# Token norms of the input from a second load of x with tokens on the partitions, and their factors in two multiplications

## The chip, the cores and the metric

The kernel runs on one core of a Trainium2 chip. The core has TensorE (matrix products, written PE in the profile, its weight loads PEld), VectorE (DVE), ScalarE (ACT), GpSimd (POOL) and SyncE (SP), which here only issues transfers; 16 DMA engines move data between the chip's memory and the on-chip memory of 128 partitions. Each engine works through its own queue in order and waits on semaphores. The metric is the device time of one execution in microseconds (us); the median of three runs before the change is 2240.29 us (2239.57 to 2240.89).

## The reference

One inference step of a one-layer encoder on 1024 prompt tokens and 64 sample tokens of width 1024. What matters here is its head:

```
def rms_norm(x, g=None):
    y = xf * lax.rsqrt(jnp.mean(xf * xf, axis=-1, keepdims=True) + EPS)
    ...
rq, rk, rv, rg, sq, sk, sv, ga, gb = jnp.split(rms_norm(x, g_attn) @ w_in, ...)
q, k, v = retention_qkv(rq, rk, rv, pos)          # rotary on q and k
s = einsum('bihd,bjhd->bhij', q, k) * intra       # decay inside a chunk
o = s @ v + (q @ state) * q_dec
new_state = state * exp(log_gamma * C) + (k * k_dec)^T @ v
```

Each token's row of x is divided by the root of its mean square. A projection is linear, so the kernel multiplies by the gain g_attn before the projections and applies the token's factor 1/root afterwards, where it needs it: to v and the scores of retention by token, and to the other projections as a row over all partitions. Behind the head follow the four-head retention, a sliding-window attention, two gated branches, cross attention, a SwiGLU block and a last norm.

## The kernel before

All 1088 tokens are held as columns, the 1024 features as 8 tiles of 128 partitions (KT = 8), in two halves of HALF = 544 tokens. Products are in fp32 as three passes of a high and a low part (`split`, lines 122 to 124: a cast on ScalarE, a difference on VectorE). The big projections go through one step of Strassen's scheme (`strassen`, line 247): seven products, each of four weight tiles and both quarters of a half, into pairs of PSUM banks `pq`; VectorE adds them up into `u` (line 252) and `stage` (line 571), and by that frees the banks for later products.

The order of instructions on each engine is not written out: the tile framework plans it with a timeline simulated at build time (line 94), from program order, dependencies and planned durations, with a few hints (`high_priority`, `issue_after`). SyncE's queue takes nearly all loads and stores, each with its wait for the buffer or the data in front, so a load that waits holds up those behind it.

`project_phase` (line 546) is the stage around the change. After the first product of values it opens a pool `ra`, loads the rotary table `rope`, and for the first head projects and rotates k (`rotated`, line 590: VectorE's adds at line 571, its four multiplications at lines 602 to 605, GpSimd's sum and difference at 606 and 607, stores to `d_qkv` in memory), calls `token_squares`, projects and rotates q, calls `token_roots` and `retention_setup`, and then `retention(0)` (line 702), which loads k, v and q from `d_qkv` in blocks of 256 tokens. The planner runs the projections of the next head among the retention's blocks.

- `token_squares` (line 448): for each half and each of the 8 feature tiles a load of 128 x 544 from `xT` into a tile `xsq`, whose buffers are those of four retention tiles not yet in use (tags kt, vb, ss, st); ScalarE squares it in place (line 457; the first of a half straight into `rstd`), VectorE adds it to `rstd` (line 459). After that `rstd` holds, for each token's column, 128 partial sums.
- `token_roots` (line 461): nine small products of `rstd` with ones on TensorE (line 468; the profile counts two instructions for each) turn them into a sum per token with tokens on the partitions, in `pt`; the steps of `rsqrt` (lines 289 to 294, on VectorE but for a root on ScalarE) make `rtok`, 128 x 9, in two sets, for eight columns of 128 tokens and one of 64.
- `retention_setup` (line 676): the factors of tokens for 4 heads and 2 kinds (decay of k, decay of the output), `tok`, from `rtok` and the tables `tab`: for each head and kind one multiplication for eight columns (line 684) and one for the last (line 686); one more instruction forms a square (line 688).
- `spread_roots` (line 472) later writes `rtok` as a row over all partitions into `rstd`.

In retention, `kt` (lines 730, 731) takes `tok`, `vb` (739, 740) and the scores' scaling (751) take `rtok`; the scores `pss` (line 746, three passes at lines 149 to 151) need q's load `qs`, its cast on ScalarE and its difference on VectorE.

Of the kernel before, what the change touches and what calls it, by code (L numbers as in the profile page):

```python
# [11 lines left out]
F32 = mybir.dt.float32  # L12
F32R = mybir.dt.float32r
AF = mybir.ActivationFunctionType
ALU = mybir.AluOpType
# [4 lines left out]
P = 128  # L20
D = 1024
KT = D // P
SEQ = 1024
SMP = 64
T = SEQ + SMP
# [4 lines left out]
H = 4  # L30
# [10 lines left out]
HALF = T // 2  # L41
# [68 lines left out]
class Kernel:  # L110
# [336 lines left out]

    def token_squares(self):

        nc, tags = self.nc, ("kt", "vb", "ss", "st")  # L450
        for t in range(2):
            hs = slice(t * HALF, (t + 1) * HALF)
            for k in range(KT):
                x = self.ra.tile([P, HALF], F32, tag=tags[k % 4], bufs=1, name="xsq")
                self.load(x, self.io["xT"][k, :, hs])
                acc = self.rstd[:, hs]
                nc.scalar.activation(x if k else acc, x, AF.Square)
                if k:
                    nc.vector.tensor_tensor(out=acc, in0=acc, in1=x, op=ALU.add)

    def token_roots(self):

        nc = self.nc
        ps = self.norm_psum("pt")
        pv = ps[:, :18].rearrange("p (t two) -> p t two", two=2)
        for i in range(9):
            w = P if i < 8 else SMP
            nc.tensor.matmul(pv[:w, i, :], self.rstd[:, i * P:i * P + w], self.ones[:, :2], start=True, stop=True)
        self.rsqrt(self.rtok[:, :8], pv[:, :8, 0], D)
        self.rsqrt(self.rtok[:SMP, 8:], pv[:SMP, 8:, 0], D)  # L470

    def spread_roots(self):

# [202 lines left out]
    def retention_setup(self):  # L676

        nc, tab = self.nc, self.tab
        self.load(tab[:, 0], self.io["c_kdec"])
        self.load(tab[:, 1], self.io["c_gdec"])  # L680
        for h in range(H):
            for i in range(2):
                v = lambda x: x.rearrange("p (b two) -> p b two", two=2)
                nc.vector.tensor_tensor(out=v(self.tok[:, i, h, :8]), in0=v(self.rtok[:, :8]),
                                        in1=tab[:, i, h, :2].unsqueeze(1).broadcast_to([P, 4, 2]), op=ALU.mult)
                nc.vector.tensor_tensor(out=self.tok[:, i, h, 8:], in0=self.rtok[:, 8:], in1=tab[:, i, h, 2:], op=ALU.mult)
        f = self.tok[:, 1].rearrange("p h t -> p (h t)")
        nc.vector.scalar_tensor_tensor(self.tok[:, 2].rearrange("p h t -> p (h t)"), f, 1.0 / 256, f, ALU.mult, ALU.mult)

# [1013 lines left out]
```

## Time and profile before

| | |
|---|---|
| median of the runs | 2240.29 us |
| the profiled execution | 2244.47 us, its span 2242.7 us |
| granted TensorE clock, mean | 0.988 |
| TensorE busy | 2168.9 us |
| VectorE busy | 1596.0 us |
| ScalarE busy | 885.4 us |
| GpSimd busy | 692.1 us |
| moved by DMA | 290.86 MB |

The profile follows one execution. Its page gives the busy time of each engine with the share of the span, the chain of work that ended last, and the costliest groups of instructions with the mean duration of one and the engine's idle time in front of them. Views of the trace cut it to a stretch: waits (who waited for whom: total, times, longest), instructions in order of time (start, duration, engine, line, output<-inputs), groups by line or by tile (count, shortest/median/longest in ns), and busy time by windows, whose rows give the window, its length, busy time and count of each engine, the granted clock, the DMA engines' busy share and GB/s. A name such as `xsq` is a tile of the program, L459 a line of it, SPq the sequencer that issues transfers. Consecutive instructions of one engine overlap a little, so that the step from one start to the next is shorter than the duration.

### The profile page before, as it was taken

How to read it: one execution, taken by the hardware profiler on the slowest of the kernel's cores; microseconds unless marked ns; L12 is line 12 of the kernel's file. 1: busy time of each engine (PE TensorE's matmuls, PEld its weight loads, DVE VectorE, ACT ScalarE, POOL GpSimd, SP SyncE). 2: the span in 40 equal slices, each digit the busy share in tenths (PEclk: the TensorE clock that was granted, in tenths of full speed). 3: DMA queues.
4: the chain of work that ended last, by engine and by line, in shares of the span. 5: the costliest groups of instructions: out<-in, count | busy, mean ns of one | idle time of the engine just before them, and what ended most of it. 6: DMA issues, size and time to landing. Idle time of an engine off the chain costs nothing.

```text
span 2242.7 us, 41756 instructions
## 1 busy us (share of the span) xinstructions
PE 2168.9 (97%) x16434; PEld 2105.3 (94%) x16434; DVE 1596.0 (71%) x2655; ACT 885.4 (39%) x1897; POOL 692.1 (31%) x466
## 2 busy tenths in 40 slices
PE   8899999999999989999999999999999999999986
PEld 8899999999999977779999998999999999999986
DVE  7986878666687667776455556668777677778587
ACT  7333333435444355554133333333323222344243
POOL 1441533342253112220000000014556555434462
PEclk9999999999999999999999999999999999999998
DMA  5533445443445475326443111422333332475233
GB/s 193 163 108 114 118 124 136 133 126 114 167 151 181 150 229 163 114 69 211 132 152 101 64 46 59 138 89 88 121 129 102 102 120 90 147 267 184 85 98 108
DMA packets 182599, 290.86 MB, mean 130 GB/s; under 512 B 40290, under 2 KB 110850, under 8 KB 182402
## 3 DMA queue, kind: packets, MB, share of 16 engines
q1 hardware_dynamic: 177794, 279.26, 39.3%
q10 hardware_dynamic: 4608, 8.91, 1.1%
q8 instruction: 130, 2.13, 0.4%
q14 instruction: 67, 0.55, 0.1%
HBM read 196.95 MB, written 91.16 MB: 128 GB/s over the span
## 4 chain that ended last, share of the span: by engine, by line
PE 79%; DVE 11%; DMA 5%; issue 2%; ACT 2%; POOL 1%; SPq 0%; DVEq 0%; ACTq 0%; POOLq 0%
PE pq L208 15%; PE pq L206 15%; PE pq L205 15%; PE pd L149 8%; PE pd L151 8%; PE pd L150 8%; DVE wq L124 2%; PE pout L1006 1%; DMA hl<-d_op 1%; PE pp L990 1%; PE pss L948 1%; DVE T L124 1%; DVE B L124 1%; DVE xg L1294 1%; DMA qs<-d_qkv 1%
## 5 line engine op out<-in xcount | busy, mean ns | idle before, releaser
L124 DVE TENSOR_TENSOR wq<-raw,wq 128x512 fp32r<-128x512 f32 (+1 forms) x505 | 448.8, 893 | 125.2 <-ACT wq L123 122.0
L123 ACT CAST wq<-raw 128x512 fp32r<-128x512 f32 (+1 forms) x505 | 307.5, 614 | 568.0 <-PE pq L208 259.1
L205 PE MATMUL pq<-T,wq 128*128 128x272 f32 x1832 | 492.9, 289 | 6.8 <-DVE u L252 3.6
L206 PE MATMUL pq<-T,wq 128*128 128x272 f32 x1832 | 493.0, 289 | 0.0
L206 PE MATMUL pq<-B,wq 128*128 128x272 f32 x1592 | 428.9, 289 | 9.1 <-DVE B L124 9.1
L205 PE MATMUL pq<-B,wq 128*128 128x272 f32 x1592 | 427.1, 289 | 0.2 <-ACT B L123 0.2
L208 PE MATMUL pq<-T,wq 128*128 128x272 f32 x1832 | 384.5, 290 | 3.4 <-DVE wq L124 3.4
L183 POOL TENSOR_TENSOR raw<-raw 128x512 f32<-128x512 f32 (+1 forms) x59 | 80.1, 1357 | 897.2 <-DVE rs_r L291 485.7
L205 PEld LDWEIGHTS pq<-T,wq 128*128 128x128 f32 x1832 | 346.1, 189 | 7.9 <-DVE u L252 3.7
L206 PEld LDWEIGHTS pq<-T,wq 128*128 128x128 f32 x1832 | 345.9, 189 | 0.3 <-issue 0.3
L208 PE MATMUL pq<-B,wq 128*128 128x272 f32 x1592 | 333.9, 290 | 0.0
L206 PEld LDWEIGHTS pq<-B,wq 128*128 128x128 f32 x1592 | 300.4, 189 | 11.0 <-DVE B L124 10.7
L205 PEld LDWEIGHTS pq<-B,wq 128*128 128x128 f32 x1592 | 300.2, 189 | 0.9 <-issue 0.4
L208 PEld LDWEIGHTS pq<-T,wq 128*128 128x128 f32 x1832 | 291.2, 190 | 4.6 <-DVE wq L124 3.8
L208 PEld LDWEIGHTS pq<-B,wq 128*128 128x128 f32 x1592 | 252.9, 190 | 0.5 <-issue 0.3
L252 DVE TENSOR_TENSOR u<-pq,u 128x544 f32<-128x544 f32 x177 | 127.6, 721 | 109.7 <-PE pq L208 109.2
L186 POOL TENSOR_TENSOR raw<-raw 128x512 f32<-128x512 f32 (+1 forms) x59 | 85.5, 1449 | 127.3 <-DVE wq L124 124.7
L976 POOL TENSOR_TENSOR t<-t,den 128x768 f32<-128x768 f32 (+2 forms) x34 | 47.9, 1408 | 170.7 <-DVE den L974 44.4
L571 DVE TENSOR_TENSOR stage<-pq,u 128x544 f32<-128x544 f32 x112 | 80.4, 718 | 26.4 <-PE pq L208 25.4
L184 POOL TENSOR_TENSOR raw<-raw 128x512 f32<-128x512 f32 (+1 forms) x59 | 87.3, 1480 | 3.7
L1461 POOL TENSOR_TENSOR y<-u,y 128x544 f32<-128x544 f32 x38 | 62.6, 1656 | 72.6 <-DVE y L1459 50.5
L189 POOL TENSOR_TENSOR raw<-raw 128x512 f32<-128x512 f32 (+1 forms) x59 | 83.3, 1412 | 4.4
(373 smaller groups left out, 4677.0 us busy)
## 6 DMA issues: line engine op xcount, KB each, us to landing
hl<-d_op SPq DMA_DIRECT2D x85, 272.0 KB, 4.6
d_qkv<-stage SPq DMA_DIRECT2D x44, 272.0 KB, 2.3
d_op<-stage SPq DMA_DIRECT2D x44, 272.0 KB, 2.4
d_op<-ht SPq DMA_DIRECT2D x44, 272.0 KB, 3.3
raw<-w_gate SPq DMA_DIRECT2D x22, 512.0 KB, 3.5
raw<-w_up SPq DMA_DIRECT2D x22, 512.0 KB, 3.6
d_gate<-stage ACTq DMA_DIRECT2D x32, 272.0 KB, 2.7
raw<-w_down SPq DMA_DIRECT2D x16, 512.0 KB, 4.2
```

Source lines behind the costliest of these rows:

```text
L123: self.last_cast = self.nc.scalar.copy(hi, src).ins
L124: return self.nc.vector.tensor_tensor(out=lo, in0=src, in1=hi.bitcast(F32), op=ALU.subtract).ins
L149: mm(ps, wh, xh, start=start, stop=False)
L150: mm(ps, wh, xl, start=False, stop=False)
L151: self.last_mm = mm(ps, wl, xh, start=False, stop=stop).ins
L184: tt(out=a21, in0=a21, in1=a22, op=add)
L186: tt(out=a11, in0=a22, in1=a11, op=sub)
L189: tt(out=a12, in0=a12, in1=a11, op=sub)
L205: mm(ps[:, c, :HC], w[:, 0, ks], x[:, 0, cs], start=start, stop=False)
L206: mm(ps[:, c, :HC], w[:, 0, ks], x[:, 1, cs], start=False, stop=False)
L208: self.last_mm = mm(ps[:, c, :HC], w[:, 1, ks], x[:, 0, c * HC:(c + 1) * HC], start=False, stop=stop).ins
L252: add = lambda out, a, b: nc.vector.tensor_tensor(out=out, in0=a, in1=b, op=ALU.add)
```

## The change

The host hands x over a second time, untransposed (`x_tok`, 1088 x 1024). `token_squares` loads it in nine tiles with tokens on the partitions, 128 x 1024 (the last has 64 tokens), in three buffers (tags kt, vb, st; the one of ss is too small for 1024 columns). ScalarE squares each in place and writes the sum over its columns into a column of `rtok`. The adds on VectorE and the products with ones are gone, and `rstd` is first written by `spread_roots`. `token_roots` is one set of root steps over the nine columns, in place (in the last column the 64 lanes without a token hold 1.0 from line 350 and are not used). `retention_setup` forms the factors of both kinds and all heads in one multiplication for eight columns and one for the last.

```diff
     def token_squares(self):
 
-        nc, tags = self.nc, ("kt", "vb", "ss", "st")
-        for t in range(2):
-            hs = slice(t * HALF, (t + 1) * HALF)
-            for k in range(KT):
-                x = self.ra.tile([P, HALF], F32, tag=tags[k % 4], bufs=1, name="xsq")
-                self.load(x, self.io["xT"][k, :, hs])
-                acc = self.rstd[:, hs]
-                nc.scalar.activation(x if k else acc, x, AF.Square)
-                if k:
-                    nc.vector.tensor_tensor(out=acc, in0=acc, in1=x, op=ALU.add)
+        tags = ("kt", "vb", "st")
+        for i in range(9):
+            w = min(P, T - i * P)
+            x = self.ra.tile([P, D], F32, tag=tags[i % 3], bufs=1, name="xsq")[:w]
+            self.load(x, self.io["x_tok"][i * P:i * P + w])
+            self.nc.scalar.activation(x, x, AF.Square, accum_out=self.rtok[:w, i:i + 1])
 
     def token_roots(self):
 
-        nc = self.nc
-        ps = self.norm_psum("pt")
-        pv = ps[:, :18].rearrange("p (t two) -> p t two", two=2)
-        for i in range(9):
-            w = P if i < 8 else SMP
-            nc.tensor.matmul(pv[:w, i, :], self.rstd[:, i * P:i * P + w], self.ones[:, :2], start=True, stop=True)
-        self.rsqrt(self.rtok[:, :8], pv[:, :8, 0], D)
-        self.rsqrt(self.rtok[:SMP, 8:], pv[:SMP, 8:, 0], D)
+        self.rsqrt(self.rtok, self.rtok, D)
...
         self.load(tab[:, 0], self.io["c_kdec"])
         self.load(tab[:, 1], self.io["c_gdec"])
-        for h in range(H):
-            for i in range(2):
-                v = lambda x: x.rearrange("p (b two) -> p b two", two=2)
-                nc.vector.tensor_tensor(out=v(self.tok[:, i, h, :8]), in0=v(self.rtok[:, :8]),
-                                        in1=tab[:, i, h, :2].unsqueeze(1).broadcast_to([P, 4, 2]), op=ALU.mult)
-                nc.vector.tensor_tensor(out=self.tok[:, i, h, 8:], in0=self.rtok[:, 8:], in1=tab[:, i, h, 2:], op=ALU.mult)
+        n = 2 * H
+        tok, tab = (x.rearrange("p i h t -> p (i h) t") for x in (self.tok[:, :2], tab))
+        nc.vector.tensor_tensor(out=tok[:, :, :8].rearrange("p n (b two) -> p n b two", two=2),
+                                in0=self.rtok[:, :8].rearrange("p (b two) -> p b two", two=2).unsqueeze(1).broadcast_to([P, n, 4, 2]),
+                                in1=tab[:, :, :2].unsqueeze(2).broadcast_to([P, n, 4, 2]), op=ALU.mult)
+        nc.vector.tensor_tensor(out=tok[:, :, 8], in0=tab[:, :, 2], in1=self.rtok[:, 8:].broadcast_to([P, n]), op=ALU.mult)
...
     arr["xT"] = np.ascontiguousarray(x.T).reshape(KT, P, T)
+    arr["x_tok"] = x
```

## The prediction, made before the changed kernel was run

> **What bounds the kernel now.** I read the page first: the shares of the engines, then the chain that ended last.
>
> ```profile
> PE 2168.9 (97%) x16434; PEld 2105.3 (94%) x16434; DVE 1596.0 (71%) x2655; ACT 885.4 (39%) x1897; POOL 692.1 (31%) x466
> ...
> PE 79%; DVE 11%; DMA 5%; issue 2%; ACT 2%; POOL 1%; SPq 0%; DVEq 0%; ACTq 0%; POOLq 0%
> ```
>
> TensorE works 2168.9 of 2242.7 us, so only 74 us of it stand still, and an edit on another engine is worth at most the TensorE waits that it removes. Which waits lie where the change works shows in the busy time by windows: the stretch from the first loads of xsq to the first retention block, the two long holes in it with the time right behind each, and the rest of the retention stage.
>
> ```profile
> 55.00:125.00 70.00, 61.58 (x468) 60.84 (x468) 66.74 (x108) 26.43 (x47) 33.32 (x20) 0.95 0.45 144
> 77.60:81.20 3.60, 0.00 (x0) 0.00 (x0) 3.60 (x5) 1.14 (x2) 1.71 (x1) 1.00 1.00 338
> 82.00:85.30 3.30, 3.30 (x17) 3.30 (x16) 3.30 (x6) 1.82 (x3) 1.42 (x1) 0.51 0.92 322
> 111.25:114.70 3.45, 0.00 (x0) 0.00 (x0) 1.18 (x2) 0.61 (x2) 2.28 (x2) 1.00 0.34 99
> 116.20:119.60 3.40, 3.40 (x19) 3.40 (x18) 3.40 (x7) 0.45 (x1) 1.56 (x1) 0.50 0.11 15
> 115.00:575.00 460.00, 453.56 (x3598) 443.07 (x3598) 343.66 (x618) 193.05 (x416) 158.47 (x106) 1.00 0.42 123
> ```
>
> The columns are the window, its length, the busy time of PE, PEld, DVE, ACT and POOL, the granted clock, the DMA share and GB/s. Between 55 and 125 us VectorE is busy 66.74 of 70 us and TensorE misses 8.42. Behind each hole of some 3.5 us the granted clock is 0.51 and 0.50 for 3.3 and 3.4 us, so a hole costs another 3.3 x 0.49 = 1.6 and 3.4 x 0.50 = 1.7 us. In the 460 us after that TensorE misses only 6.4. The waits of TensorE in this stretch, from the view of waits:
>
> ```profile
> PE pq L205 <- DVE u L252: 3.6, 1, 3.6
> PE pss L149 <- ACT qs L123: 3.5, 1, 3.5
> PE pq L205 <- DVE stage L571: 0.6, 1, 0.6
> PE pk L699 <- issue: 0.6, 1, 0.6
> ```
>
> These four are the whole 8.42 us (3.6 + 3.5 + 0.6 + 0.6). The first is VectorE being late; in the chain of waits cut to the first 240 us the adds that the change removes are a line of their own, and in VectorE's order of time the late instruction stands right behind them:
>
> ```profile
> by line: PE pq L208 9.4%; PE pq L205 9.3%; PE pq L206 9.1%; issue 6.9%; DVE wq L124 4.9%; DMA xr<-xT 4.2%; DVE rstd L459 4.1%; DVE xg L1294 3.5%; DVE T L124 3.4%; DMA qs<-d_qkv 3.3%; DVE stage L571 2.7%; DVE stage L603 2.5%; DVE B L124 2.4%
> ...
> 78.70 1.85 DVE L459 TENSOR_TENSOR rstd<-rstd,xsq 128x544 f32<-128x544 f32 x1
> 80.47 0.71 DVE L252 TENSOR_TENSOR u<-pq,u 128x544 f32<-128x544 f32 x1
> ```
>
> TensorE waits from 77.6 to 81.2 for the add at 80.47, which frees a pair of PSUM banks; an add of squares that takes 1.85 us stands right in front of it.
>
> **The change, part by part.** *The adds of squares (L459) go.* Their row, grouped by line and form, and an undisturbed one in order of time:
>
> ```profile
> L459 DVE TENSOR_TENSOR rstd<-rstd,xsq 128x544 f32<-128x544 f32 x14 | 14.3, 1028 | 0.1
> ...
> 81.71 0.71 DVE L459 TENSOR_TENSOR rstd<-rstd,xsq 128x544 f32<-128x544 f32 x1
> 82.34 0.71 DVE L571 TENSOR_TENSOR stage<-pq,u 128x544 f32<-128x544 f32 x1
> ```
>
> VectorE gets back 14.3 us as measured. The lower end is 14 x 0.63 = 8.8 us: an undisturbed add begins at 81.71 and the next instruction at 82.34; 5.5 us of the 14.3 are stretched adds, and what stretches them may stretch their successors. The Trainium skill (SBUF — State Buffer, section Who interferes with whom) says that a VectorE instruction with two SBUF inputs and a GpSimd instruction that reads SBUF exclude each other for a whole instruction; by that rule the stretch moves to the next such instruction, the relief is 8.8 and the sum is the one below, while a relief of 14.3 would bring q's rotation 5.5 earlier and close the second hole too, for the sum of the first rival. I take 8.8 because GpSimd's own work stays. It is enough, by the windows of line 459 alone ahead of the hole's end:
>
> ```profile
> 52.00:81.00 29.00, 10.29 (x9) 1.00 0.67 215
> ```
>
> Nine of the adds lie there, at least 9 x 0.63 = 5.7 us against the 3.6 of the wait. So I take away the whole first hole: 3.6 + 1.6 for the low clock = 5.2, and the two short waits, 1.2 together, the first of which names VectorE, the second nothing (the low end there is 0.6).
>
> *The products with ones (L468) go from TensorE.*
>
> ```profile
> 92.27 1.24 PE L468 MATMUL pt<-ones,rstd 128*128 128x2 f32 x10
> 93.44 0.66 PE L699 MATMUL pk<-ident,ks 128*128 128x128 f32 x4
> ...
> L468 PE MATMUL pt<-ones,rstd x18: 168/252/252, 77.1 to 93.3; 128*128 128x2 f32 x16, 128*64 128x2 f32 x2
> ```
>
> Ten of them take 92.27 to 93.44, 0.117 each, 18 take 2.1 us, all on TensorE's own path. The other end is 1.2: the eight ahead of the first hole (8 x 0.117 = 0.9) count nothing if that hole stays, which with the adds gone it does not.
>
> *Squares on ScalarE: 16 of 544 columns become 9 of 1024 with a sum.*
>
> ```profile
> L457 ACT ACTIVATE xsq<-xsq x14: 655/658/662, 53.1 to 86.2; 128x544 f32<-128x544 f32 x14
> L819 ACT ACTIVATION_READ_ACCUMULATOR ret_o<-po x32: 192/197/205, 125.8 to 553.8; 128x1 f32 x32
> ...
> 120.29 0.51 ACT L123 CAST ss<-sf 128x384 fp32r<-128x384 f32 x1
> 120.87 0.62 ACT L123 CAST ks<-ks 128x512 fp32r<-128x512 f32 x1
> ```
>
> 128 more columns cost 0.11 us in the casts, so 480 cost 0.41 and a square about 0.66 + 0.41 + 0.20 for reading the sum = 1.27; nine are 11.4 against 16 x 0.66 = 10.6 now. ScalarE is busy 26.43 of the 70 us, so +0.8 is hidden behind its idle time; were that cover gone it would cost 0.8.
>
> *Loads: 16 of 272 KB in four buffers become nine (the last of 64 rows) of 512 KB in three.* The bytes are the same 4.4 MB. From the groups of DMA issues and the queues' waits:
>
> ```profile
> xsq<-xT SPq DMA_DIRECT2D x16, 272.0 KB, 4.9
> raw<-w_q SPq DMA_DIRECT2D x4, 512.0 KB, 3.8
> ...
> SPq L117 <- DVE rstd L459: 18.6, 9, 7.1
> ...
> ACT xsq L457 <- DMA xsq<-xT: 7.8, 7, 2.5
> ```
>
> Today SyncE's queue stands 18.6 us behind loads whose buffer waits for an add of VectorE, and with it the weight loads and the stores of d_qkv behind it. After the change the buffer waits for the square alone. A round of three loads needs about 4.9 + 1.27, so three rounds 18.5 us, against the 33 from 53.1 to 86.2 that the squares span now. What can get worse is ScalarE standing in front of a larger load with the casts of weights behind it: one more wait of 2.5, the longest now, to 4.9, a full landing. Behind it the casts of q's weights have room, by ScalarE's order of time:
>
> ```profile
> 55.88 1.14 ACT L123 CAST wq<-raw 128x512 fp32r<-128x512 f32 x2 [0.66 <-DVE rstd L459]
> ...
> 69.86 0.60 ACT L255 COPY u<-pq 128x544 f32<-128x544 f32 x1
> ```
>
> The first two weights are cast at 55.9 and q's first product is copied out at 69.9. So I take nothing; ends: -2.5 (the longest wait of ScalarE goes, and TensorE behind it gains that) and +3.5, one more hole as above without its clock.
>
> *Roots and factors.*
>
> ```profile
> L684 DVE TENSOR_TENSOR tok<-rtok,tab x8: 157/159/168, 105.1 to 106.2; 128x8 f32<-128x8 f32 x8
> L686 DVE TENSOR_TENSOR tok<-rtok,tab x8: 150/152/154, 105.3 to 106.2; 128x1 f32<-128x1 f32 x8
> L688 DVE SCALAR_TENSOR_TENSOR tok<-tok x1: 185/185/185, 107.1 to 107.1; 128x36 f32<-128x36 f32 x1
> ```
>
> Sixteen factors from 105.1 on, the last begun at 106.2, take 1.2 us; two, of 64 and 8 columns, are near the 0.185 of the 36-column row, 0.35 together. One set of root steps instead of two saves a few steps of 0.07 (sixteen in 1.2 us). That is 1.2 us of VectorE ahead of 110, on the way to q's round trip only, and counted there.
>
> *What is late next: q's round trip.* The second hole is a product of the first retention block that waits for q, which goes over memory:
>
> ```profile
> 102.95 2.04 POOL L607 TENSOR_TENSOR stage<-stage 128x544 f32<-128x544 f32 x1
> 108.53 0.33 SPq L117 DMA_DIRECT2D raw<-w_q  x1
> 108.97 1.38 SPq L117 DMA_DIRECT2D qs<-d_qkv  x1
> 114.09 0.62 ACT L123 CAST qs<-qs 128x512 fp32r<-128x512 f32 x1 [5.21 <-DMA qs<-d_qkv]
> ```
>
> From GpSimd's last piece of q's rotation to the cast are 11.1 us: that piece, the store, SyncE's queue with w_q's load in front, and the landing (108.97 to 114.09). VectorE's part ends earlier by at least the 8.8; TensorE arrives earlier by 3.6 + 1.6 + 1.2 + 2.1 = 8.5. Both move alike, so I keep the second hole and its low clock as they are: 0, with ends of -5.2 (it closes) and +6.4 (q moves only 2.1).
>
> **The sum.** 5.2 + 1.2 + 2.1 = 8.5 us off. The profiled execution took 2244.5 us (span 2242.7 and 1.8 around it), and so 2236.0; it is 4.2 above the median of the runs, 2240.3, which gives 2231.8 there.
>
> **The rivals.** *Both holes close.* For it: after the change SyncE no longer stands behind the adds, and VectorE is done with q sooner. Against it: the order on TensorE is set by the planner's own times, which already put that product 3.5 us too early. Then 8.5 + 3.5 + 1.7 = 13.7 off: 2226.6. The Trainium skill (TensorE: Matmul & The Clock Gate, Part 1: The HAM clock gate) lets the clock fall only after an idle window of about 3.4 us; by that rule a second hole shortened by 0.2 alone gives back its 1.7 of low clock, 10.4 off in all. The trace agrees so far: holes of 3.6 and 3.5 have the low clock behind them, those of 0.6 have none.
>
> *The gain is handed back.* TensorE comes to the second hole 8.5 earlier, but GpSimd's 2.04, the store, the wait for w_q's buffer and the landing of 5.1 don't shorten, and the first hole's time reappears there. Against it: that chain starts at VectorE, which is the engine relieved. If only the 2.1 us of removed products survive: 2238.2.
>
> *Slower: more holes like the second.* The order of the whole retention stage is worked out anew from planned times. With the factors known earlier, blocks can be set earlier on TensorE than their loads from d_qkv land. Each such wait has the price of the one seen, 3.5 + 1.7 = 5.2; the second more than eats the 8.5, and three (one for each further block of the first head) make +7.1: 2247.4. For it: the one block at the front shows it now. Against it: in 115 to 575 us, with 15 further blocks, TensorE misses 6.4 us in all.
>
> That the change would not do what it says I give no case: the squares' adds have no other place in the new code.
>
> **How the numbers follow.** Forecast as summed: 0.42. Both close: 0.18. Handed back: 0.22. Slower: 0.18. Of 2240, 0.2% is 4.5 us, about what a measurement of this kernel can tell from no change. The forecast (own range 2228.5 to 2235.5, by the second hole growing or shrinking by 3.5) and the closing are faster, 0.60; handed back is the same, with the two-wait form of the slower case, 0.23; 0.17 slower. Range 2226 to 2243: it takes in the closing, the handing back and the forecast, and leaves out the slower case's 2247.
>
> **What would show it.** Right: no adds on rstd and no pt products before 100 us; VectorE idle at times between 55 and 110; the wait of pq for u at 77 us gone and no clock of 0.51 behind it; TensorE's waits in 55 to 125 us are one of some 3.5 for qs. Wrong: a wait of TensorE for a cast behind a square (ScalarE idle for xsq's landing over 4 us), or waits of pss for qs in several blocks, or a sum of waits up to 575 us no smaller than today's.

## The result, and the profile after

The changed kernel takes 2246.26 us (median of 11 runs, 2241.73 to 2249.46); the kernel before, on the same chip, 2241.55 us (11 runs, 2236.71 to 2248.87). The ratio is 1.0019, 95% interval 1.0010 to 1.0028: slower by 2.2 to 6.3 us, where 8.5 us less had been predicted. The profiled execution took 2244.28 us with a span of 2242.5 us, the one of before 2244.47 and 2242.7. Single executions of one kernel range over 8 to 12 us, so two spans can't be set against each other; a stretch of the trace can, as will be seen. One of the twelve runs of e2 below was 5% longer at a granted clock of 0.84 and is left out of its ratio.

The page of the changed kernel, its busy times and the chain that ended last:

```profile
PE 2168.6 (97%) x16416; PEld 2103.9 (94%) x16416; DVE 1590.0 (71%) x2622; ACT 884.0 (39%) x1898; POOL 690.9 (31%) x466
...
PE 81%; DVE 10%; DMA 4%; issue 2%; ACT 2%; POOL 1%; SPq 0%; DVEq 0%; ACTq 0%; POOLq 0%
```

The 18 instructions of the products with ones are gone from PE. Busy time by windows of the changed kernel, the two stretches of the prediction:

```profile
55.00:125.00 70.00, 60.41 (x461) 59.34 (x460) 56.64 (x73) 27.31 (x53) 32.61 (x20) 0.95 0.40 136
115.00:575.00 460.00, 450.78 (x3572) 440.45 (x3572) 345.07 (x613) 191.33 (x413) 159.22 (x106) 1.00 0.41 122
```

VectorE is relieved by 10.1 us in the 70 (66.74 to 56.64), more than the 8.8 taken. Yet TensorE misses more in both stretches: 9.6 us instead of 8.4, and 9.2 instead of 6.4. The waits of TensorE in the changed kernel, to 125 us and from 125 to 600, and then the one row of before that answers to the last of them:

```profile
PE pss L149 <- ACT qs L123: 4.4, 1, 4.4
...
PE pq L205 <- DVE rs_t L293: 2.1, 1, 2.1
PE pq L208 <- DVE wq L124: 1.9, 1, 1.9
...
PE pq L205 <- ACT u L255: 0.9, 1, 0.9
...
PE pb L818 <- ACT ret_o L814: 8.0, 4, 2.8
```

```profile
PE pb L829 <- ACT ret_o L825: 5.1, 4, 1.5
```

The wait of 3.6 us for `u` is gone. In its place stand two of about 2 us, the hole for `qs` has grown from 3.5 to 4.4, and a wait of 2.8 us for the block's scaled output `ret_o` is new. The same in TensorE's order of time (start, duration, and in brackets the idle time in front with what ended it):

```profile
72.58 0.52 PE L208 MATMUL pq<-T,wq 128*128 128x272 f32 x2 [1.95 <-DVE wq L124]
86.41 0.36 PE L205 MATMUL pq<-T,wq 128*128 128x272 f32 x1 [2.08 <-DVE rs_t L293]
111.33 0.58 PE L149 MATMUL pss<-qs,ks 128*128 128x256 f32 x1 [4.43 <-ACT qs L123]
135.20 0.44 PE L818 MATMUL pb<-ident,ret_o 128*128 128x128 f32 x2 [2.80 <-ACT ret_o L814]
165.79 0.44 PE L818 MATMUL pb<-ident,ret_o 128*128 128x128 f32 x2 [1.97 <-ACT ret_o L814]
```

**A stretch as a ruler.** I set the two programs' instructions side by side. By source line, tiles and shape, TensorE's instructions in the two traces (16,434 and 16,416) come in the same order but for 69 of before and 51 of the changed kernel: the 18 of the products with ones, and some 50 that stand at another place, all between 77 and 152 us. So the change acts ahead of that, and in it. I measure from TensorE's first product with a T operand of w_k (near 49 us) to the first scores `pss` of block 0, on to the transposes `pb` of block 0's output, and on to those of block 1. For the changed kernel these stand at 49.04, 111.33, 135.20 and 165.79. All times in us:

| kernel | to scores | to output 0 | to output 1 | sum | ratio to before, 95% interval |
|---|---|---|---|---|---|
| before | 64.98 | 19.08 | 29.87 | 113.93 | |
| changed | 62.29 | 23.87 | 30.59 | 116.75 | 1.0019 [1.0010, 1.0028] |
| e0 changed, again | 62.27 | 23.87 | 30.58 | 116.72 | 1.0017 [1.0004, 1.0031] |
| e1 squares alone | 61.92 | 20.22 | 29.88 | 112.02 | 0.9988 [0.9977, 0.9998] |
| e2 factors alone | 64.13 | 23.27 | 30.30 | 117.70 | 1.0011 [0.9999, 1.0024] |
| e4 changed, no squares | 57.28 | 23.29 | 30.30 | 110.87 | 0.9995 [0.9984, 1.0006] |
| e5 squares behind casts, old factors | 61.92 | 19.44 | 29.87 | 111.23 | 0.9999 [0.9988, 1.0010] |
| e6 changed, one load | 60.03 | 21.74 | 30.36 | 112.13 | one run, 2239.95 us |
| e7 changed, short squares | 60.81 | 23.81 | 30.32 | 114.94 | one run, 2245.15 us |
| e8 changed, squares behind casts | 60.78 | 23.20 | 30.34 | 114.32 | 1.0009 [1.0000, 1.0019] |
| e9 changed, loads behind w_q's | 59.05 | 24.30 | 28.90 | 112.25 | 1.0004 [0.9992, 1.0016] |
| e10 loads behind w_q's, old factors | 62.17 | 19.70 | 30.14 | 112.01 | 0.9990 [0.9978, 1.0001] |
| e11 loads and squares behind, old factors | 61.46 | 18.92 | 30.16 | 110.54 | 0.9984 [0.9973, 0.9995] |
| e12 the same, again | 59.64 | 19.60 | 30.15 | 109.39 | 0.9988 [0.9979, 0.9997] |

So the change gained 2.7 us up to the first scores and lost 4.8 and 0.7 behind them: 2.8 slower in the stretch, inside the 2.2 to 6.3 of the runs. Two questions follow: what costs 5.5 us in the first retention blocks, and why only 2.7 of 8.5 us came up to the scores.

### The profile page after: what moved, and what is told of

It reads as the page before. It is cut to its first block, busy times and chain, and to the rows that moved or that the text cites. A ratio compares the mean times of both kernels' runs of the same rounds, so it can differ in the third digit from the quotient of the medians.

```text
span 2242.5 us, 41669 instructions
## 1 busy us (share of the span) xinstructions
PE 2168.6 (97%) x16416; PEld 2103.9 (94%) x16416; DVE 1590.0 (71%) x2622; ACT 884.0 (39%) x1898; POOL 690.9 (31%) x466
## 4 chain that ended last, share of the span: by engine, by line
PE 81%; DVE 10%; DMA 4%; issue 2%; ACT 2%; POOL 1%; SPq 0%; DVEq 0%; ACTq 0%; POOLq 0%
PE pq L208 15%; PE pq L206 15%; PE pq L205 15%; PE pd L149 8%; PE pd L151 8%; PE pd L150 8%; DVE wq L124 2%; PE pout L995 2%; PE pp L979 1%; DMA hl<-d_op 1%; PE pss L937 1%; DVE stage L560 1%; DVE B L124 1%; DVE stage L592 1%; PE pk L688 1%
## 5 line engine op out<-in xcount | busy, mean ns | idle before, releaser
L124 DVE TENSOR_TENSOR wq<-raw,wq 128x512 fp32r<-128x512 f32 (+1 forms) x505 | 453.5, 903 | 136.5 <-ACT wq L123 134.3
L206 PEld LDWEIGHTS pq<-B,wq 128*128 128x128 f32 x1592 | 301.3, 189 | 10.5 <-DVE B L124 10.1
```

The lines of the kernel that those rows point to most:

```text
L124: return self.nc.vector.tensor_tensor(out=lo, in0=src, in1=hi.bitcast(F32), op=ALU.subtract).ins
L206: mm(ps[:, c, :HC], w[:, 0, ks], x[:, 1, cs], start=False, stop=False)
```

## The experiments

The early expectations measure the first part from ScalarE's copy of w_k's first product. That copy turned out to stand anywhere from 1.95 us ahead of the T product to 0.38 behind it, so the table starts at TensorE's own instruction; the four values that the expectations quote as 64.8, 62.7, 62.3 and 56.9 are 65.0, 62.3, 61.9 and 57.3 in it.

**e0: the changed kernel once more.** No edit.

> The changed kernel once more, to see what of its two traces repeats. Order theory (the re-planned order of the first retention block makes TensorE wait for that block's output, and this costs more than the adds gave): ratio to the kernel before 1.001 to 1.003, and the waits of TensorE in 45 to 170 us as in the first trace: about 4.4 for qs, 2.8 and 2.0 for ret_o. Chance theory (the two traces differ by one run's luck): ratio around 1.000 and other waits.

1.0017 again, and each part of the stretch repeats to 0.02 us. The loss isn't chance. (That a repeat can also differ shows below: e12 is the program of e11 and takes 1.8 us less to the scores.)

**e1: the new squares with the old factors.**

```diff
-        self.rsqrt(self.rtok, self.rtok, D)
+        self.rsqrt(self.rtok[:, :8], self.rtok[:, :8], D)
+        self.rsqrt(self.rtok[:SMP, 8:], self.rtok[:SMP, 8:], D)
...
+        (retention_setup as before the change: sixteen multiplications)
```

> Squares by the new load on ScalarE, but the roots in two sets and the sixteen factors as before. The planner then sets TensorE's instructions from the first block's output on as in the kernel before. Order theory: the wait of the first block's output (2.8 us and the low clock behind it, some 4.3) is gone and the gain of the adds shows: 2 to 6 us faster than before. Load theory (the 512 KB loads and the squares hold up the weights): no better than the changed kernel, 3 to 5 us slower than before. Nothing-gained theory (VectorE's time was never TensorE's): within 2 us of before.

**e2: the new factors with the old squares.** Only `retention_setup` is that of the change.

> Only the factors in two multiplications; squares, adds, products with ones and loads as before. The planner then sets TensorE's instructions from the first block's scores on as in the changed kernel. Order theory: slower than before by 2 to 6 us, with a wait of TensorE of 2 to 3 us for ret_o near 135 us that the kernel before has not. Load and nothing-gained theory: within 2 us of before, since 1 us of VectorE is all that goes.

The transposes of block 0's output, in e1 and then in e2:

```profile
131.29 0.44 PE L819 MATMUL pb<-ident,ret_o 128*128 128x128 f32 x2 [1.06 <-ACT ret_o L815]
```

```profile
134.99 0.44 PE L829 MATMUL pb<-ident,ret_o 128*128 128x128 f32 x2 [2.82 <-ACT ret_o L825]
```

The part of the change that I costed at nothing, beyond 0.35 us of VectorE, carries the loss. With the old factors TensorE's order from the first scores on is that of before (but for eight instructions in e1, and wholly in e5 and e10 to e12 below), the block takes 20.2 us, and the kernel is faster than before (0.9988). With the new factors and nothing else the block takes 23.3 us and shows the wait of 2.8; the time of e2, 1.0011 [0.9999, 1.0024], would not show it by itself. Three pairs of kernels differ by this edit alone (with the roots in one set or two): e2 and before, the changed kernel and e1, e8 and e5. Behind the scores it costs 4.6, 4.4 and 4.2 us. Idle time of TensorE is 2.9, 2.1 and 1.2 of these, and nearly all the rest is low clock behind the holes, which goes partly by chance, as the last section shows. The factors themselves are as cheap as predicted: 0.22 and 0.17 us for the two multiplications. What they do is to let the planner set the block's order anew: twelve more instructions of the next head's projections, 1.5 us of work, now stand between the scores and the output (151 against 139 of TensorE), and the output still isn't ready.

Why it isn't shows in VectorE's order of time. The chain from `rv` to `rr` is seven small steps. In the changed kernel, with what stands between the steps, and ScalarE's scaling as the last row:

```profile
125.76 0.15 DVE L811 TENSOR_TENSOR rv<-rv,tok 128x2 f32<-128x2 f32 x1
125.83 0.71 DVE L560 TENSOR_TENSOR stage<-pq,u 128x544 f32<-128x544 f32 x1
126.47 1.39 DVE L593 TENSOR_TENSOR stage<-stage,rope 128x544 f32<-128x544 f32 x1
127.79 0.15 DVE L289 TENSOR_SCALAR rs_v<-rv 128x2 f32<-128x2 f32 x1
127.86 0.68 DVE L124 TENSOR_TENSOR wq<-raw,wq 128x512 fp32r<-128x512 f32 x1
128.46 1.88 DVE L592 TENSOR_TENSOR stage<-stage,rope 128x544 f32<-128x544 f32 x1
...
130.38 0.73 DVE L594 TENSOR_TENSOR stage<-stage,rope 128x544 f32<-128x544 f32 x1
131.02 1.32 DVE L292 TENSOR_TENSOR rs_t<-rr 128x2 f32<-128x2 f32 x1
132.26 0.68 DVE L124 TENSOR_TENSOR wq<-raw,wq 128x512 fp32r<-128x512 f32 x1
132.87 1.28 DVE L293 SCALAR_TENSOR_TENSOR rs_t<-rs_t,rs_v 128x2 f32<-128x2 f32 x1
...
134.38 0.16 DVE L298 TENSOR_TENSOR rr<-rr,tok 128x2 f32<-128x2 f32 x1
...
134.63 0.91 ACT L814 ACTIVATE ret_o<-ret_o,rr 128x256 f32<-128x256 f32 x2 [5.43 <-DVE rr L298]
```

and in the kernel before:

```profile
126.38 0.60 DVE L822 TENSOR_TENSOR rv<-rv,tok 128x2 f32<-128x2 f32 x1 [0.65 <-ACT ret_o L819]
126.90 0.71 DVE L571 TENSOR_TENSOR stage<-pq,u 128x544 f32<-128x544 f32 x1
...
128.22 0.71 DVE L603 TENSOR_TENSOR stage<-stage,rope 128x544 f32<-128x544 f32 x1
128.85 0.68 DVE L124 TENSOR_TENSOR wq<-raw,wq 128x512 fp32r<-128x512 f32 x1
...
129.53 1.81 DVE L605 TENSOR_TENSOR stage<-stage,rope 128x544 f32<-128x544 f32 x1
...
131.44 1.34 DVE L293 SCALAR_TENSOR_TENSOR rs_t<-rs_t,rs_v 128x2 f32<-128x2 f32 x1
...
133.02 0.16 DVE L298 TENSOR_TENSOR rr<-rr,tok 128x2 f32<-128x2 f32 x1
```

From `rv` to `rr` it takes 8.6 us instead of 6.6: six instructions of the next head stand between the steps, 6.1 us of work, instead of four with 3.9; one more multiplication of the rotation and one more split. (The steps themselves sum to the same 3.3 to 3.4 us in both kernels, though two of them take 1.3 us instead of 0.15 here, and one there.) And `rv` begins late: before, at 126.38, as soon as ScalarE has its sums (126.34); in the changed kernel at 125.76, 2.0 us after ScalarE's (123.79), behind two multiplications and a split of the next head. These 2.0 and 2.0 us, and 0.9 by which ScalarE's sums come later behind the scores (the low clock there is 0.7 longer), are the block's 4.8. So the chain ends 1.4 us later in absolute time, while TensorE, which reached the scores 3.4 us earlier, has run out of work ahead of it.

**e4: the changed kernel with neither loads nor squares.** `token_squares` is empty, so the norms of tokens are left out.

> The changed kernel without the nine loads and squares at all (the roots are taken of a constant, so the tokens' norms are left out of the result); TensorE's order is that of the changed kernel. Order theory: as slow as the changed kernel, 1.001 to 1.003, with the waits for qs and ret_o still there. Load theory: the holes near 72, 86 and 111 us go and it is 5 to 9 us faster than the changed kernel. Nothing-gained theory: within 2 us of before.

The order of TensorE from 44 us on is that of the changed kernel, and the block takes 23.3 us, near its 23.9. The hole for `qs` stays too (3.95 us). But the scores stand 57.28 us behind the first product instead of 62.29, and the holes near 72 and 86 us are gone; the time, 0.9995, is some 5 us under that of the changed kernel. So the loads and squares, costed at nothing, hand back 5.0 us. Not they alone: the roots, which wait for nothing here, are taken in the first 5 us of the kernel and the factors at 13.7, so that their steps leave the stretch as well. The next four kernels ask which part of the loads and squares does it.

**e5 and e8: the first squares behind w_q's second cast on ScalarE**, with the old factors (e5) and with the new ones (e8). In the changed kernel the first three squares, which wait 2.0 us for a load, stand ahead of these casts.

```diff
...
+                    w = pair("w_q", h)
                     if h == 0:
-                        self.token_squares()
-                    rotated(pair("w_q", h), h, 0)
+                        with tc.issue_after(self.casts[1]):
+                            self.token_squares()
+                    rotated(w, h, 0)
```

> The new squares with the old factors, and the first squares queued on ScalarE behind w_q's second cast instead of ahead of it; nothing of the computation is left out. Stretch one goes from ScalarE's copy of w_k's first product (line 255) to the first scores of block 0: before 64.8 us, the changed kernel 62.7, the new squares with the old factors 62.3, without squares and loads 56.9. Stretch two goes from there to the transposes of block 0's output: 19.1, 23.9, 20.2, 23.3. Cast theory (the squares' harm is that ScalarE waits for their loads with w_q's casts queued behind): stretch one falls to 57 to 60, stretch two stays near 20, and the time is 0.995 to 0.998 of before. Work theory (ScalarE's 11 us of squares are the harm wherever they stand) and load theory (the 4.4 MB of loads are): stretch one stays at 61.5 to 63.5 and the time at 0.998 to 1.000.

> The changed kernel with the first squares queued behind w_q's second cast; TensorE's order is that of the changed kernel to the last instruction. Cast theory: stretch one falls from 62.7 to 57 to 60. Work and load theory: 61.5 to 63.5. Order theory: stretch two keeps its 23 to 24, so that the time stays above the same edit with the old factors by some 4 us, at 0.998 to 1.001 of before.

To the scores e5 takes 61.92, just what e1 takes, and e8 60.78, 1.5 less than the changed kernel. Against the 57 to 60 expected the cast theory falls as the main cause. e5's time (0.9999) is no better than e1's either.

**e6: one load and nine squares of it; e7: nine loads and squares of 16 columns.**

```diff
e6
-            self.load(x, self.io["x_tok"][i * P:i * P + w])      (in the loop)
+        self.load(x, self.io["x_tok"][:P])                       (once, ahead of it)
...      (the squares go to two other tiles)
e7
-            self.nc.scalar.activation(x, x, AF.Square, accum_out=...)
+            self.nc.scalar.activation(x[:, :16], x[:, :16], AF.Square, accum_out=...)
```

> The changed kernel with one load of x's first 128 tokens instead of nine, and nine squares of that tile, so that the tokens' norms are those of the first tile throughout (eight loads left out). Load theory: stretch one (copy of w_k's first product to the first scores of block 0) falls from 62.7 to 57 to 58, as without squares. Work theory: it stays at 62 to 63.5. Cast theory: ScalarE no longer waits for loads, but four squares in a row, 5 us, stand ahead of w_q's third cast: 58 to 62. Stretch two (to the transposes of block 0's output) is 23 to 24 by the order theory, since TensorE's order is that of the changed kernel.

> The changed kernel with all nine loads, but squares of only the first 16 columns of each tile, so that the sums leave out the other columns. Work theory: stretch one (copy of w_k's first product to the first scores of block 0) falls from 62.7 to 57 to 58. Load theory: it stays at 62 to 63.5. Cast theory: ScalarE still waits for the first three loads with w_q's casts behind, but loses only about 0.35 us a square: 60 to 62. Stretch two is 23 to 24 by the order theory.

60.03 and 60.81: neither the bytes nor ScalarE's time is the cause by itself; each makes the stretch 1.5 to 2.3 us shorter, in one trace each, and neither reaches the 57.3 of e4. Both traces have 1.7 us of low clock ahead of the scores, where the changed kernel and e4 have none; by TensorE's idle time in the stretch alone they are nearer to e4 (5.9 and 6.6 us, against 9.6 in the changed kernel, 7.6 in e8 and 4.7 in e4). What these kernels share shows on VectorE and GpSimd. In the changed kernel (the fourth row is GpSimd's first piece of w_q):

```profile
55.24 0.72 DVE L252 TENSOR_TENSOR u<-pq,u 128x544 f32<-128x544 f32 x1 [1.34 <-PE pq L208]
58.23 0.72 DVE L252 TENSOR_TENSOR u<-pq,u 128x544 f32<-128x544 f32 x1 [2.27 <-PE pq L208]
...
59.51 1.28 DVE L124 TENSOR_TENSOR wq<-raw,wq 128x512 fp32r<-128x512 f32 x2
...
60.32 1.62 POOL L183 TENSOR_TENSOR raw<-raw 128x512 f32<-128x512 f32 x1 [11.44 <-DVE wq L124]
```

and in e4:

```profile
55.59 1.28 DVE L124 TENSOR_TENSOR wq<-raw,wq 128x512 fp32r<-128x512 f32 x2
...
57.23 1.29 POOL L183 TENSOR_TENSOR raw<-raw 128x512 f32<-128x512 f32 x1 [8.49 <-DMA raw<-w_q]
```

VectorE's first two splits of w_q stand behind an add on `u` that waits 2.27 us for TensorE. The casts were done by 57.2; the splits begin at 59.51, GpSimd 3.1 us later than in e4, and the weights of w_q's later products come so late that TensorE waits 1.95 us at 72.58. This order is the same in e0, e1, e5, e6, e7 and e8, and so is that hole (1.93 to 1.95 us, in e6 2.77). The first three loads of `xsq` stand ahead of w_q's in SyncE's queue (in e6 the only one). My guess is that the planner reckons with that and so puts the splits late; its plan isn't shown.

**e9: the loads behind w_q's loads**, all else as changed. TensorE's order is that of the changed kernel.

```diff
...
+                        with tc.issue_after(wq_loaded):
+                            self.token_squares()
```

> The changed kernel with the loads of xsq queued on SyncE behind w_q's two loads; nothing of the computation is left out, and TensorE's order is that of the changed kernel to the last instruction. I take the stretch from TensorE's first product with a T operand of w_k (near 49 us) to the first scores of block 0: before 65.0 us, the changed kernel 62.3, with the first squares behind w_q's second cast 60.8, with one load 60.0, with short squares 60.8, without squares and loads 57.3. In all of these but the last, VectorE has w_q's first two splits behind an add on u that waits 2.3 us for TensorE, and GpSimd's first piece of w_q begins at 60.1 to 61.0 instead of 57.2. Split theory (the loads set ahead of w_q's in the plan push those splits behind that wait, and the rest follows): with w_q's loads first the splits come before 57.5, GpSimd's piece before 58.5, the hole of 1.95 us near 72.6 is gone, and the stretch is 57.5 to 60. Load and work theories (bytes, or ScalarE's 11 us): the stretch stays at 61 to 63. Order theory: from the scores to the transposes of block 0's output it stays at 23 to 24 us.

```profile
56.96 1.28 DVE L127 TENSOR_TENSOR wq<-raw,wq 128x512 fp32r<-128x512 f32 x2
59.31 0.72 DVE L255 TENSOR_TENSOR u<-pq,u 128x544 f32<-128x544 f32 x1 [1.06 <-PE pq L211]
...
58.87 1.29 POOL L186 TENSOR_TENSOR raw<-raw 128x512 f32<-128x512 f32 x1 [8.74 <-DMA raw<-w_q]
```

The splits stand ahead of the waiting add now, GpSimd begins 1.45 us earlier (at 58.87, a little later than expected), the holes at 72.58 and 86.41 are gone, and the scores stand at 59.05: 3.2 of the 5.0 us come back. For the hole of 1.95 us at 72.58 the split theory holds: it is away here and in e4 and e10 to e12, wherever the splits come ahead of the waiting add. The hole of 2.08 us at 86.41 is another matter, since it is away in e6, e7 and e8 too, with the splits late. In the changed kernel the add on `u` that ends it (at 85.55) stands behind a root step of 1.23 us (84.40) and a split that waited 2.64 us for its cast (81.29); which of these decides stays open. The block behind keeps its 24.3 us, as the order theory says. The time is 1.0004 [0.9992, 1.0016].

**e10, e11, e12: both causes undone.** Old factors, and the loads behind w_q's first load (e10), or behind its second with the squares behind w_q's fourth cast (e11; e12 is e11 again).

```diff
e10
...
+                        with tc.issue_after(wq_loaded):                               (w_q's first load)
e11, e12
...
+                        with tc.issue_after(wq_loaded), tc.issue_after(self.casts[3]):  (its second)
+                            self.token_squares()
```

> The new squares with the old factors, and the loads of xsq behind w_q's first load; nothing of the computation is left out, and TensorE's order of the first retention block is that of before. Split theory and order theory together: the stretch to the first scores is 57.5 to 60.5 us (61.9 with the loads ahead), from there to the transposes of block 0's output 19 to 20.5, and the time 0.995 to 0.998 of before. If the split theory is wrong: 61 to 63 and 0.998 to 1.000.

> As the kernel with the loads behind w_q's and the old factors, but with the loads behind w_q's second load and the squares behind w_q's fourth cast on ScalarE; nothing of the computation is left out, and TensorE's order of the first retention block is that of before. Split theory: the stretch to the first scores is 57.5 to 60.5 us and the time 0.995 to 0.998 of before; if the squares' place on ScalarE matters as well, it is some 0.5 to 1 us better than with the loads alone. If the split theory is wrong: 61 to 63 and 0.998 to 1.000.

> The kernel with the old factors, the loads of xsq behind w_q's second load and the squares behind w_q's fourth cast, once more, to see whether its 0.9984 [0.9973, 0.9995] of before holds, since it is the lowest of several ratios. By the trace (3.4 us less than before from w_k's first product with a T operand to the transposes of block 1's output): 0.998 to 0.999. If that ratio was the chance of one draw: 0.999 to 1.001. The stretch itself repeats: 61.3 to 61.7 us to the first scores, 18.8 to 19.1 to the transposes of block 0's output.

The blocks behave as expected (18.9 to 19.7 to the output). The part ahead of them does not: e11 takes 61.46 instead of 57.5 to 60.5, with a low clock in it that the last section prices, and e10 stays at 62.17 with the splits early. A new wait took the place, in VectorE's and TensorE's order:

```profile
78.57 0.20 DVE L295 RECIPROCAL rtok<-rtok 128x8 f32<-128x8 f32 x1 [1.38 <-ACT rtok L294]
78.69 0.67 DVE L256 TENSOR_TENSOR u<-pq,u 128x544 f32<-128x544 f32 x1
...
79.41 0.39 PE L209 MATMUL pq<-T,wq 128*128 128x272 f32 x1 [3.67 <-DVE u L256]
```

The steps of the roots now come early on VectorE, wait there for ScalarE's last squares and its root (in front of which stands a table load of 1.28 us at 77.03), and the add that frees the PSUM banks stands behind them: the first hole of the old kernel is back at its old place and size, with no add of squares left. In e11 and e12 it is away; their one long hole is another, 4.3 us at 103 for a `stage`. e11 is 0.9984 [0.9973, 0.9995] of before, and e12 0.9988 [0.9979, 0.9997], so this version beats the kernel before by about 3 us and, by the ratios, the changed one by about 7. All three ratios (e10's is 0.9990) lie above the 0.995 to 0.998 expected of e10 and e11. The stretch of e12 was expected to repeat e11's, with 61.3 to 61.7 to the scores and 18.8 to 19.1 behind, and took 59.64 and 19.60; that miss is taken up in the last section.

## Why the prediction was wrong

**What held.** The adds and products left as said. The wait of 3.6 us at 77 and its low clock are gone: the granted clock is 1.00 in every window from 49 to 106.9 us. Nine squares take what was worked out, and the two factors too; the squares, with the reading of their sums and the loads' times to landing, in the changed kernel:

```profile
L455 ACT ACTIVATE xsq<-xsq x9: 1044/1057/1065, 52.2 to 74.1; 128x1024 f32<-128x1024 f32 x8, 64x1024 f32<-64x1024 f32 x1
L455 ACT ACTIVATION_READ_ACCUMULATOR xsq<-xsq x9: 183/184/189, 53.2 to 75.1; 128x1 f32 x8, 64x1 f32 x1
...
DMA to landing us min/median/max: 3.6/6.4/7.4
```

1.06 + 0.18 = 1.24 us against 1.27. ScalarE waited for `xsq` once, for 2.0 us, far under the 4 that would have been the sign of harm: the harm came without that sign. Another sign of being wrong did come: TensorE's waits are no smaller than before but larger, in both stretches.

**The books.** Against before, up to block 1's output: the products with ones 2.1 off. TensorE's holes went from 9.9 us (3.64 + 0.63 + 0.64 + 3.51 and 1.49 at block 1) to 14.4 (1.95 + 2.08 + 0.94 + 0.20 + 4.43 + 2.80 + 1.97): 4.5 more. The low clock went from 1.7 + 1.7 to 2.4 + 1.7 (6 us at 0.60 behind the scores, and 5.8 us behind 135.20, below): 0.7 more. Together 3.1 slower; the stretch says 2.8. Up to the scores alone, all the 8.5 that were summed came off, but new holes of 1.95, 2.08, 0.94 and 0.20 and the 0.9 more for `qs` took 6.1 back: 2.4 are left, and the stretch says 2.7. (A slip of 0.2 in the prediction, on which nothing hangs: 2231.8 with 3.5 either way is 2228.3 to 2235.3.)

**Steps that failed.**

- *"So I take nothing", for the loads and squares.* They hand back 5.0 us (e4, where the roots leave the stretch as well), above the end of +3.5. I looked at ScalarE and at the queue of SyncE, where the wait for the buffer of `xsq` did improve (18.6 us to 9.6), and priced the work by what is queued behind it on its own engine. The price arose on VectorE. The loads' place alone costs 3.2 (e9): the hole of 1.95 goes with w_q's splits, which the planner put behind an add that waits for TensorE, and that of 2.08 by a way that stays open. Of the other 1.8 these runs don't say which part is the squares, the loads or the roots.
- *The first hole, 5.2 us, "with the adds gone it does not" stay.* It went, but e10 shows that the adds weren't its only possible cause: 3.67 us at the same instruction, with another wait in front of `u`. Work removed ahead of a late instruction makes it early only if nothing else that waits is set there.
- *"Both move alike", for the second hole.* TensorE came to the scores 4.4 us earlier (it stands from 106.90 instead of 111.25), q's cast 3.4 (110.65 instead of 114.09), so the hole grew by 0.9 and its low clock by 0.7. VectorE's 8.8 us did not arrive at q: GpSimd's last piece of q's rotation began at 101.57 instead of 102.95, 1.4 us earlier.
- *Factors and roots at 0.35 and "counted there".* The right duration (0.22 + 0.17), the wrong kind of cost. e2 shows 3.8 us slower in the stretch from this edit alone, and the three pairs 4.2 to 4.6 behind the scores: with the new factors the planner sets more of the next head's work ahead of the first block's output and inside the chain that makes it.
- *The slower rival* named the mechanism, an order worked out anew with the factors known earlier, at 0.18. It put the waits at `pss` for q in several blocks; there is still one of those. The wait came instead at the end of the first block, `pb` for `ret_o`, once with 2.80 us in place of none. That its time, 2247.4, is near the measured 2246.3 is luck: it kept all of the 8.5 and added three waits of 5.2. *Handed back* comes near for the part up to the scores (2.7 of 8.5; it had 2.1), also by luck: new holes on the way took the gain, and not GpSimd, the store and the landing.

Of the Trainium skill (SBUF — State Buffer, Who interferes with whom) the prediction used that a two-input instruction of VectorE is stretched by GpSimd's, so that the stretch moves to the next one. The trace agrees in so far as the multiplication at 128.46 takes 1.88 us, where undisturbed ones take 0.71, while GpSimd's instruction from 127.94 runs 1.82. But the kernel before has such a one in the chain of `rr` as well (1.81 us at 129.53), so it is the two more instructions, and not the stretching, that lengthened the chain.

## What to carry to other kernels

Where a planner orders the instructions, price an edit also by what its new durations and new early results let the planner move: here sixteen tiny instructions made into two cost 4.2 to 4.6 us at another place. Compare the orders of the two programs before trusting any sum, and hold unneeded early work behind the loads and casts that TensorE will want next. When a load is added, look not only at who queues behind it on its engine but at where the following casts, splits and adds land on the others, and at which of these sit behind an instruction that waits.

## What was not expected of the hardware

The clock's price of a hole is not settled by its length. Behind the new hole of 2.80 us the changed kernel shows a low clock, after more than a microsecond at full speed; the windows of the hole and of the time behind it:

```profile
132.40:135.20 2.80, 0.00 (x1) 0.01 (x1) 2.64 (x5) 0.57 (x2) 1.73 (x1) 1.00 0.65 202
135.20:137.00 1.80, 1.80 (x14) 1.80 (x15) 1.07 (x3) 1.32 (x3) 0.00 (x0) 0.90 0.73 285
137.00:139.00 2.00, 2.00 (x11) 2.00 (x10) 1.97 (x4) 0.62 (x1) 0.00 (x0) 0.50 0.57 180
139.00:141.00 2.00, 2.00 (x14) 2.00 (x13) 2.00 (x5) 0.47 (x1) 0.00 (x0) 0.73 0.59 219
```

That is 0.2 + 1.0 + 0.5 = 1.7 us, and the prediction had counted low clock only for holes of some 3.5 us. At a finer cut the clock is 0.50 from 136.66 to 140.07 and 1.00 on both sides. In all fourteen traces the low clock behind these holes comes in such pieces, of 3.41 us or twice that, which within an execution begin at multiples of 3.41 us from one another: one piece costs 1.7 us, and what of a piece falls into the hole itself costs nothing. The six microseconds behind a hole of 4.30 us in e11, behind the same hole (4.32 us) in e12, and behind one of 3.05 us in e5:

```profile
103.60:109.60 6.00, 6.00 (x26) 6.00 (x27) 4.61 (x7) 1.27 (x3) 2.70 (x2) 0.50 0.42 134
```

```profile
103.05:109.05 6.00, 6.00 (x36) 6.00 (x37) 4.90 (x7) 1.77 (x3) 2.97 (x2) 0.72 0.40 134
```

```profile
110.85:116.85 6.00, 6.00 (x48) 5.84 (x48) 6.00 (x10) 3.27 (x6) 2.83 (x3) 1.00 0.31 90
```

The same hole of the same program cost 3.0 us of clock in one execution and 1.7 in the other; that is most of the 1.8 us by which their stretches differ. One of 3.05 us cost nothing. The Trainium skill (TensorE: Matmul & The Clock Gate, Part 1: The HAM clock gate) says that the gate watches a window of about 3.4 us that runs on freely, whatever the kernel does. That the price changes from run to run fits this; that a hole of 2.80 us, shorter than the window, had one does not fit a rule of a window wholly idle, by which the prediction's first rival reckoned. In e7 even the hole of 1.93 us ahead of 72.31 had one (0.50 from 72.56 to 75.97), where the same hole of 1.95 in the changed kernel had none; in e9 a hole of 2.80 had none. Over the stretch in the fourteen traces, holes of 2.8 to 4.5 us carry 1.6 to 3.0 us of clock, and two of them none. Which it will be can't be read from the hole's length, and that may be part of why single executions of one kernel scatter; this is not shown.
